# Latent attention heads: scores with keys on partitions, and float32 exponentials straight into float32 value products

## The chip, the cores and the metric

The kernel runs on one core of a Trainium2 chip. A core has five engines, each working through its own list of instructions in a fixed order: TensorE (PE, matrix products and transposes into PSUM), VectorE (DVE), ScalarE (ACT), GpSimd (POOL) and SyncE (SP), which here issues the DMA transfers. They wait for one another by semaphores. The metric is the device time of one execution in microseconds (us). The profile is that of one execution. Its page names instructions by the line of the kernel and by the tiles that they write and read (`pvm<-PTm,vt`: into `pvm` from `PTm` and `vt`). PEld is the loading of weights into TensorE, which can lie beside products.

## What is computed

One encoder layer on 1,024 positions of width 1,024, in float32: a modulated norm; one input projection; two groups of eight heads side by side, latent attention and chunk attention; one output projection; then a norm and a gated MLP. The change concerns the latent heads alone. For each of the eight heads, with queries and keys of 96 and values of 64:

```python
q = rmsnorm(q, g_mla_q[l]); k = rmsnorm(k, g_mla_k[l])      # then rotary on the last 32
s = jnp.einsum('bqhd,bkhd->bhqk', qi, k) * scale
mask = key_chunk[None, :] <= q_chunk[:, None]               # chunks of 64
s = jnp.where(mask[None, None], s, NEG_INF)
p = jax.nn.softmax(s, axis=-1)
return jnp.einsum('bhqk,bkhd->bqhd', p, v)
```

A query thus sees all keys up to the end of its own chunk of 64.

## The kernel before

The stages follow one another: norm and modulation of the input; chunk attention, with its projections and those of the latent group as fillers; latent attention; output projection and second norm; up-projection with convolution and gate, tile by tile; down-projection.

Float32 numbers go through TensorE in two pieces, a rounded one (`hi`, type fp32r, one pass per product) and a remainder (`lo`), and a product is the sum of three: hi by hi, hi by lo, lo by hi (`gemm3`). A plain float32 operand is also possible; in the profile such a product is two instructions.

A latent head is worked on in two units, `g` = 0 for the queries 0 to 511 and `g` = 1 for 512 to 1,023. For each unit `prep` makes a page of its queries and one of its keys (`qk_page`): four transposes into one PSUM bank (tag `T`, one buffer), the rounded piece by ScalarE, the remainder by VectorE. A unit has four tiles of 128 queries. `scores(i)` puts one tile's scores into PSUM with queries on partitions and up to 1,024 keys beside one another (tag `S`, two buffers, three passes, negated by the gain `gk_m`); VectorE masks the last chunk (memset) and reduces each row to its minimum; ScalarE takes the exponential with that minimum as bias and sums the rows. VectorE turns the sums into reciprocals, POOL scales the exponentials by them and rounds them to half precision, VectorE writes the remainder in half precision (`hl`), and SP issues a DMA transpose that puts keys on partitions (`PT`). `values(i)`, three tiles later (`DEPTH`), multiplies these pieces of 128 by 128 with a half-precision value tile that holds the rounded value and its remainder side by side (`vt`), so that `pv` (one PSUM bank) gets one half from the rounded values and one from the remainders. After four tiles ScalarE copies one half, VectorE adds the other, and SP writes the result to `oT_d`. The values carry a power of two worked out from the weights (`pow2_scale`).

Queries, keys and values of four heads come from `f_up(0)` and `f_up(1)`: per tile of 128 positions two small products (`qu`, `ku`) and a chain of norms and rotary steps, most of them on VectorE. These, and `f_oca`, the half of the output projection that belongs to the chunk heads (tiles `oc`), are fillers: generators from which `pace` takes a step whenever the attention work before it has paid for it, and `need` as many as a unit requires. `f_up(1)` has to be complete before the second unit of the first head. Every instruction's place on its engine is then set by a scheduler when the kernel is built, with a raised priority for scores, exponentials and values; on the chip that order is fixed.

The second half of the output projection (tiles `op`, weights `wo`) follows the last unit, needs `oT_d` of all latent heads, and reads x and the stored partial sums again.

## Time and profile before

| | us |
|---|---|
| median of 3 runs | 1458.91 (1457.85 to 1463.05) |
| the profiled execution | 1456.23 |
| its span, first to last instruction | 1454.4 |
| PE busy | 1270.4 |
| VectorE busy | 1029.9 |
| ScalarE busy | 606.5 |
| POOL busy | 770.3 |

The latent up-projections begin at about 401 us, the last value product of the latent heads ends at about 665 us, and the output projection runs until about 734 us; from there to the end it is the MLP. Busy times of different engines overlap and don't add up. The granted clock is the share of TensorE's full speed that it was given in a stretch; the mean over the span is 0.936.

### The profile page before, as it was taken

What the parts mean: (1) busy time and instruction counts of PE and PEld (TensorE: products, weight loads), DVE (VectorE), ACT (ScalarE), POOL (GpSimd) and SP (SyncE); (2) the same over time, 40 slices, a digit from 0 to 9 for tenths busy, and PEclk for the clock granted to TensorE, in tenths of its full rate; (3) what the DMA queues carried; (4) which work ended last, traced back from release to release, by engine and by line L of the source; (5) the groups of instructions that cost most, each with busy time, mean ns of one, the idle gap of its engine ahead of it and who ended that gap; (6) DMA issues with size and microseconds to landing.
All of it is one profiled execution on the core that took longest, in us unless ns stands there. A gap on an engine that the chain in (4) does not pass through costs nothing.

```text
span 1454.4 us, 20116 instructions
## 1 busy us (share of the span) xinstructions
PE 1270.4 (87%) x6836; PEld 1054.4 (72%) x6836; DVE 1029.9 (71%) x1838; ACT 606.5 (42%) x1182; POOL 770.3 (53%) x717
## 2 busy tenths in 40 slices
PE   3859988998877789886668999999999998999997
PEld 2749877887765568675546877888888887887885
DVE  6964776576688988782577778778777776566653
ACT  4544344334455555452374343443444433322331
POOL 5363544265545764333735655556655555665662
PEclk9979997999887799997878999999999999999999
DMA  7423547555522588778712322322222234447442
GB/s 283 135 70 77 130 107 144 133 119 118 114 59 55 107 162 171 149 145 261 243 41 87 116 88 101 107 82 87 88 87 87 96 130 152 152 142 241 146 145 101
DMA packets 214627, 183.85 MB, mean 126 GB/s; under 512 B 148214, under 2 KB 179066, under 8 KB 213500
## 3 DMA queue, kind: packets, MB, share of 16 engines
q1 hardware_dynamic: 214524, 182.56, 45.3%
q8 instruction: 54, 0.88, 0.3%
q14 instruction: 49, 0.40, 0.1%
HBM read 119.07 MB, written 28.84 MB: 102 GB/s over the span
## 4 chain that ended last, share of the span: by engine, by line
PE 23%; POOL 9%; DVE 8%; issue 8%; DMA 7%; ACT 1%; SPq 1%; DVEq 0%; POOLq 0%; ACTq 0%
PE p L929 5%; PE p L931 5%; PE p L930 5%; POOL wds L82 5%; DMA wu<-w_up 2%; PE dnp L1072 2%; PE dnp L1074 2%; PE dnp L1073 2%; DVE u L1007 1%; DMA wd<-w_down 1%; DVE ws L1020 1%; DVE u L1006 1%; POOL wf L82 1%; POOL we L82 1%; POOL wd L82 1%
## 5 line engine op out<-in xcount | busy, mean ns | idle before, releaser
L82 POOL TENSOR_TENSOR wds<-wd,wds 128x512 fp32r<-128x512 f32 x88 | 152.4, 1753 | 102.7 <-ACT wds L75 102.7
L82 POOL TENSOR_TENSOR wc<-ws,wc 128x512 fp32r<-128x512 f32 x22 | 65.2, 2962 | 136.7 <-ACT wc L75 136.7
L1062 DVE TENSOR_TENSOR wd<-wd,gmbc 128x1024 f32<-128x1024 f32 x44 | 68.5, 1556 | 84.1 <-DMA wd<-w_down 84.0
L1074 PE MATMUL dnp<-wds,g 128*128 128x512 f32 x308 | 119.3, 393 | 4.6 <-DVE g L82 4.6
L1072 PE MATMUL dnp<-wds,g 128*128 128x512 f32 x308 | 120.0, 392 | 1.8 <-DVE xo L1080 1.7
L75 ACT ACTIVATE wds<-wd 128x512 fp32r<-128x512 f32 x88 | 54.8, 624 | 159.1 <-PE dnp L1074 152.3
L1073 PE MATMUL dnp<-wds,g 128*128 128x512 f32 x308 | 120.1, 391 | 0.0
L71 POOL TENSOR_SCALAR hlm<-Pm,rim 128x512 f16<-128x512 f32 (+3 forms) x96 | 64.8, 685 | 78.9 <-DVE rim L684 39.7
L71 POOL TENSOR_SCALAR hlc<-Pc,ric 128x640 f16<-128x640 f32 (+2 forms) x64 | 46.2, 724 | 80.6 <-DVE ric L684 39.5
L1020 DVE TENSOR_TENSOR ws<-wu,wu 128x512 f32<-128x512 f32 x22 | 30.5, 1387 | 75.0 <-DMA wu<-w_up 75.0
L681 ACT ACTIVATE Pc<-sc,mc 128x640 f32<-128x640 f32 (+2 forms) x64 | 42.2, 660 | 91.0 <-DVE mc L670 64.1
L655 PE MATMUL sm<-mk,mq 96*128 96x512 f32 (+3 forms) x288 | 71.2, 377 | 10.2 <-ACT Pm L681 6.7
L1006 DVE SCALAR_TENSOR_TENSOR u<-c,pk,u 128x1023 f32<-128x1023 f32 x44 | 77.4, 1766 | 1.8 <-ACT u L1005 1.8
L1041 ACT ACTIVATE u<-u 128x1024 f32<-128x1024 f32 x22 | 23.4, 1063 | 132.1 <-DVE u L1007 132.1
L655 PE MATMUL sc<-k,q 64*128 64x512 f32 (+3 forms) x288 | 68.7, 365 | 10.7 <-ACT Pc L681 6.8
L82 DVE TENSOR_TENSOR g<-gr,g 128x512 fp32r<-128x512 f32 x44 | 69.8, 1588 | 11.2 <-ACT g L75 11.2
L430 DVE SCALAR_TENSOR_TENSOR aacc<-aw,cs,aacc 128x256 f32<-128x256 f32 x84 | 44.1, 525 | 47.3 <-DMA aw<-w_ada 47.0
L1005 ACT ACTIVATE u<-c,pk 128x1024 f32<-128x1024 f32 x44 | 52.3, 1236 | 56.1 <-DVE c L1037 56.1
L705 DVE SCALAR_TENSOR_TENSOR hlm<-Pm,rim,hlm 128x512 f16<-128x512 f32 (+3 forms) x96 | 68.5, 727 | 6.1 <-POOL hlm L71 5.9
L721 PE MATMUL pvm<-PTm,vt 128*128 128x128 f16 x576 | 47.2, 232 | 28.6 <-DMA PTm<-hlm 24.5
L1074 PEld LDWEIGHTS dnp<-wds,g 128*128 128x128 f32 x308 | 58.2, 189 | 18.0 <-DVE g L82 5.9
L1072 PEld LDWEIGHTS dnp<-wds,g 128*128 128x128 f32 x308 | 58.1, 189 | 15.1 <-DVE xo L1080 2.6
(366 smaller groups left out, 4281.1 us busy)
## 6 DMA issues: line engine op xcount, KB each, us to landing
wu<-w_up SPq DMA_DIRECT2D x44, 512.0 KB, 4.5
wd<-w_down SPq DMA_DIRECT2D x44, 512.0 KB, 5.1
aw<-w_ada SPq DMA_DIRECT2D x96, 128.0 KB, 2.4
g_d<-u SPq DMA_DIRECT2D x22, 512.0 KB, 2.6
gr<-g_d SPq DMA_DIRECT2D x44, 256.0 KB, 3.6
x<-x SPq DMA_DIRECT2D x16, 512.0 KB, 6.6
adaw<-w_ada_a SPq DMA_DIRECT2D x8, 1024.0 KB, 5.2
wq_r<-w_qk SPq DMA_DIRECT2D x32, 128.0 KB, 2.8
```

What stands on the lines that cost most here:

```text
L71: pool.tensor_scalar(o, i, s, 1.0, op0=MUL, op1=MUL)
L82: (pool if eng == "p" else dve).tensor_tensor(o, i, f32(hi), op=SUB)
L655: last = pe.matmul(s[:, c:c + w], qpg[rs_, a, q], kpgs[kh][rs_, b, ko:ko + w], start=(a == 0 and b == 0), stop=(a == 1))
L705: dve.scalar_tensor_tensor(hl[:, w:2 * w], pp, ri[:], hl[:, :w], op0=MUL, op1=SUB)
L929: pe.matmul(pt, sh, pg[:, 0], start=(k == 0), stop=False)
L930: pe.matmul(pt, sh, pg[:, 1], start=False, stop=False)
L931: pe.matmul(pt, sl, pg[:, 0], start=False, stop=(k == 3))
L1006: dve.scalar_tensor_tensor(u[:, 1:], c[:, :S - 1], pk[:, cv + 1:cv + 2], u[:, 1:], op0=MUL, op1=ADD)
L1062: dve.tensor_tensor(raw[:], raw[:], gmbc[:], op=MUL)
L1072: pe.matmul(pts[t][n], sh, w[n][:, 0], start=(j == 0), stop=False)
L1073: pe.matmul(pts[t][n], sh, w[n][:, 1], start=False, stop=False)
L1074: pe.matmul(pts[t][n], sl, w[n][:, 0], start=False, stop=(j == NF - 1))
```

## The change

- `qk_page` gives the key page a 97th row, of ones (from a column of ones behind each key, gain 1.0), and the query page gets a 97th row later.
- `rows_min` takes over the row minima: for each of the unit's four query tiles one pass of the rounded pieces alone, with queries on partitions as before; mask; minimum; a transpose of the column of minima into one row of a PSUM bank (tag `T`). ScalarE then copies that row, negated, into row 97 of the query page.
- `scores(x)` now puts keys on partitions and up to 512 queries beside one another, three passes, with the 97th row in the first of them, so that the minimum is taken off in the product. A unit's causal region is cut into pieces of 512, 512 (384 and 128) and 256 columns, behind four of 512 for the keys of the first half where `g` = 1. `x` counts pairs of pieces, each pair in one buffer of tag `S`. The diagonal blocks are masked, and ScalarE writes the exponential in float32, without a bias or sums.
- `values(x)`, two pairs later, multiplies these with a float32 tile that holds the values of two heads with ones between them: `pv` gets the value sums in one half and the sum of the exponentials in the other. ScalarE copies the latter, VectorE takes the reciprocal (64 by 512) and multiplies.
- The half-precision pieces, their scaling, the DMA transposes, the power of two and the remainders of the latent values are gone. The chunk heads keep all of that (`Unit`, where only the choice between the two kinds is taken out).
- A unit is begun (`begin`: pages and minima) ahead of the scores of the unit before it.

```diff
@@ -530,12 +529,6 @@
             wq.append(w)
         raw = qtile(f"wkr{gr}")
         sp.dma_start(raw[:], I["w_kvu"][gr])
-        ssw = cst.tile([P, 1], F32, name=f"sswm{gr}")
-        junk = qtile(f"wkj{gr}")
-        act.activation(junk[:, 0:256].rearrange("p (a b) -> p a b", a=4),
-                       raw[:].rearrange("p (a b) -> p a b", a=4)[:, :, NOPE:], AF.Square, accum_out=ssw[:])
-        vscale["m", gr] = pow2_scale(f"m{gr}", ssw[:], gb2[:], 1, float(KVR))
-        sc = vscale["m", gr][0]
...
-                mq[gr, t // 2] = g3([P, 2, 4, QK], F32, f"qn{gr}_{t}")
-                mk[gr, t // 2] = g3([P, 2, 4, QK], F32, f"kn{gr}_{t}")
-                mv[gr, t // 2] = G["v"].tile([P, 2, 4, 2, 64], F16, name=f"vt{gr}_{t}", tag="Gv", bufs=8)
+                mq[gr, t // 2] = g3([P, 2, 4, QK + 1], F32, f"qn{gr}_{t}")
+                mk[gr, t // 2] = g3([P, 2, 4, QK + 1], F32, f"kn{gr}_{t}")
+                pool.memset(mk[gr, t // 2][:, :, :, QK:], 1.0)
+                if gr == 0 or t >= 6:
+                    vt = G["v"].tile([P, 2, 2, 3, 64], F32, name=f"vt{gr}_{t}", tag="Gv", bufs=5)
+                    for i in range(2):
+                        mv[gr, t + i] = vt[:, i]
+                else:
+                    for i in range(2):
+                        vt = apg.tile([P, 512], F32, name=f"vt{gr}_{t + i}", tag="v16", bufs=6)
+                        mv[gr, t + i] = vt[:, :384].rearrange("p (a b c) -> p a b c", a=2, b=3)
+                for i in range(2):
+                    pool.memset(mv[gr, t + i][:, :, 1, :], 1.0)
...
-            v_t = mv[gr, t // 2][:, t % 2]
-            act.activation(v_t[:, :, 0, :], p4[:, :, NOPE:], AF.Copy, scale=sc)
-            dve.scalar_tensor_tensor(v_t[:, :, 1, :], p4[:, :, NOPE:], sc, v_t[:, :, 0, :], op0=MUL, op1=SUB)
-            q_t = mq[gr, t // 2][:, t % 2]
+            act.activation(mv[gr, t][:, :, 0::2, :], p4[:, :, NOPE:].rearrange("p (a b) d -> p a b d", a=2), AF.Copy)
...
-                    dve.memset(sv[0:64, n - 64:n], BIG)
-                    dve.tensor_reduce(m[:], sv, axis=AX.X, op=MIN)
...
-                for x, (p0, p1) in enumerate(pieces):
-                    w = p1 - p0
-                    cnt[0] += 1
-                    spare = not u.band and cnt[0] % 2
-                    if spare:
-                        hl = apg.tile([P, 1024], F16, name=f"hl{nm}_{x}", tag="v16", bufs=6)
-                    else:
-                        hl = at.tile([P, 1280], F16, name=f"hl{nm}_{x}", tag="HL", bufs=HL_BUFS)
-                    pp = pr[:, p0:p1]
-                    mode = (MODE_C if u.band else MODE_M)[cnt[0] % 4]
-                    if mode == "2":
-                        scale_pool(pp, pp, ri[:])
-                        act.activation(hl[:, :w], pp, AF.Copy)
-                        pool.tensor_tensor(hl[:, w:2 * w], pp, hl[:, :w], op=SUB)
-                    else:
-                        if mode == "1":
-                            scale_pool(hl[:, :w], pp, ri[:])
-                        else:
-                            act.activation(hl[:, :w], pp, AF.Copy, scale=ri[:])
-                        dve.scalar_tensor_tensor(hl[:, w:2 * w], pp, ri[:], hl[:, :w], op0=MUL, op1=SUB)
-                    if spare:
-                        tt = apg.tile([P, 8, P], F16, name=f"PT{nm}_{x}", tag="v16", bufs=6)
-                    else:
-                        tt = at.tile([P, 10, P], F16, name=f"PT{nm}_{x}", tag="PT", bufs=PT_BUFS)
-                    sp.dma_start_transpose(tt[:, :2 * w // P, :], hl[:, :2 * w])
-                    u.pt[i].append((tt, lo + p0 // P, w // P))
...
+    class Latent:
+
+        def __init__(u, gr, hh, g):
+            u.gr, u.hh, u.g, u.nm = gr, hh, g, f"m{gr}{hh}"
+            u.need = ["up1"] if gr or g else ["up0"]
+            d = [[(4 * g, 0)], [(4 * g + 1, 128), (4 * g + 3, 384)], [(4 * g + 2, 256)]]
+            u.pieces = [[(kb, 0)] for kb in range(4 * g)] + d
+            u.pr = {}
+
+        def prep(u):
+            gr, hh, g = u.gr, u.hh, u.g
+            u.q = qk_page(lambda j: mq[gr, (4 * g + j) // 2][:, j % 2, hh, 0:QK], f"mq{gr}{hh}_{g}", QK, "Q", 2, None)
+            k = qk_page(lambda j: mk[gr, (4 * g + j) // 2][:, j % 2, hh, :], f"mk{gr}{hh}_{g}", QK, "K", 3, gk_m[:],
+                        QK + 1)
+            pages[gr, hh, g] = k
+            u.k = [pages[gr, hh, i] for i in range(g + 1)]
+
+        def rows_min(u):
+
+            with tc.high_priority(offset=OFF_S):
+                mt = ps.tile([P, 512], F32, name=f"mt{u.nm}_{u.g}", tag="T", bufs=TB)
+                for j in range(4):
+                    n = (4 * u.g + j + 1) * P
+                    nm = f"{u.nm}_{4 * u.g + j}"
+                    s = ps.tile([P, 1024], F32, name=f"s{nm}", tag="S", bufs=2)
+                    for c in range(0, n, 512):
+                        w = min(512, n - c)
+                        pe.matmul(s[:, c:c + w], u.q[:QK, 0, j * P:(j + 1) * P], u.k[c // 512][:QK, 0, :w],
+                                  start=True, stop=True)
+                    dve.memset(s[0:64, n - 64:n], BIG)
+                    m = cst.tile([P, 1], F32, name=f"m{nm}", tag="m", bufs=4)
+                    dve.tensor_reduce(m[:], s[:, :n], axis=AX.X, op=MIN)
+                    last = pe.transpose(mt[0:1, j * P:(j + 1) * P], m[:], ident[:])
+                act.activation(u.q[QK:QK + 1, 0], mt[0:1], AF.Copy, scale=-1.0)
+
+        def scores(u, x):
+
+            cost = 0
+            with tc.high_priority(offset=OFF_S):
+                s = ps.tile([P, 1024], F32, name=f"st{u.nm}_{u.g}_{x}", tag="S", bufs=2)
+                for y, piece in enumerate(u.pieces[2 * x:2 * x + 2]):
+                    o = 512 * y
+                    for kb, c in piece:
+                        w = 512 - c
+                        ks = slice((kb % 4) * P, (kb % 4 + 1) * P)
+                        kp = u.k[kb // 4]
+                        pe.matmul(s[:, o:o + w], kp[:QK + 1, 0, ks], u.q[:QK + 1, 0, c:], start=True, stop=False)
+                        pe.matmul(s[:, o:o + w], kp[:QK, 0, ks], u.q[:QK, 1, c:], start=False, stop=False)
+                        last = pe.matmul(s[:, o:o + w], kp[:QK, 1, ks], u.q[:QK, 0, c:], start=False, stop=True)
+                        if kb >= 4 * u.g:
+                            dve.memset(s[64:128, o:o + 64], BIG)
+                        o += w
+                        cost += 3 * max(107, w / 2.4)
+                    n = o - 512 * y
+                    tag = ("P", "HL", "PT")[len(u.pr) % 3]
+                    pr = at.tile([P, 640], F32, name=f"p{u.nm}_{u.g}_{2 * x + y}", tag=tag, bufs=3)
+                    act.activation(pr[:, :n], s[:, 512 * y:o], AF.Exp, scale=-1.0)
+                    u.pr[2 * x + y] = pr
+                trail.append(last.ins)
+            return cost
+
+        def values(u, x):
+            if x == 0:
+                u.pv = ps.tile([P, 512], F32, name=f"pv{u.nm}_{u.g}", tag="pv", bufs=1)
+            cost = 0
+            with tc.high_priority(offset=OFF_V):
+                for y in (2 * x, 2 * x + 1):
+                    if y >= len(u.pieces):
+                        break
+                    o = 0
+                    for kb, c in u.pieces[y]:
+                        w = 512 - c
+                        o2 = u.hh % 2
+                        v = mv[u.gr, kb][:, u.hh // 2, o2:o2 + 2, :].rearrange("p a b -> p (a b)")
+                        last = pe.matmul(u.pv[:, c:], v, u.pr[y][:, o:o + w], start=(kb == 0),
+                                         stop=(y == len(u.pieces) - 1))
+                        o += w
+                        cost += 4 * w / 2.4
+                trail.append(last.ins)
+                if 2 * x + 2 >= len(u.pieces):
+                    dst = at.tile([P, 512], F32, name=f"o{u.nm}_{u.g}", tag="o", bufs=1)
+                    r0, r1 = (slice(64, 128), slice(0, 64)) if u.hh % 2 else (slice(0, 64), slice(64, 128))
+                    act.activation(dst[r0], u.pv[r1], AF.Copy)
+                    dve.reciprocal(dst[r0], dst[r0])
+                    dve.tensor_tensor(dst[r0], u.pv[r0], dst[r0], op=MUL)
+                    sp.dma_start(oT_d[2 * u.gr + u.hh // 2][r0, u.g * 512:(u.g + 1) * 512], dst[r0])
+            return cost
...
+    def begin(u):
+        need(u.need)
+        u.prep()
+        u.rows_min()
...
+    wait = []
+    for n, u in enumerate(lat):
+        if n + 1 < len(lat):
+            begin(lat[n + 1])
+        for x in range(2 + 2 * u.g):
+            pace(u.scores(x), R_MLA)
+            wait.append((u, x))
+            if len(wait) > 2:
+                v, y = wait.pop(0)
+                pace(v.values(y), R_MLA)
+    for v, y in wait:
+        v.values(y)
```

91 lines of the change are left out of this document (38 added, 53 removed).

## Prediction, made before the changed kernel was run

> **What bounds the kernel now.** I read the page's head first, then the table of stretches of 50 us, then the groups of the attention stage by shape, the PE timeline, and last the SP queue at the end of that stage. The profiled execution took 1456.2 us (its span and 1.8 us around it), 2.7 us under the median of 1458.9; every sum below is made against 1456.2.
>
> ```profile
> span 1454.4 us, 20116 instructions
> 400.00:450.00 50.00, 35.98 (x163) 28.20 (x162) 43.56 (x148) 26.81 (x67) 27.67 (x30) 0.76 0.30 65
> 450.00:500.00 50.00, 38.12 (x236) 31.71 (x236) 46.84 (x144) 30.04 (x70) 30.47 (x30) 0.89 0.33 65
> 550.00:600.00 50.00, 44.50 (x313) 36.29 (x314) 38.92 (x96) 25.83 (x55) 22.24 (x29) 1.00 0.83 162
> 600.00:650.00 50.00, 44.60 (x322) 36.34 (x319) 39.44 (x107) 23.54 (x51) 16.69 (x28) 0.97 0.72 145
> 1050.00:1100.00 50.00, 50.00 (x222) 41.39 (x222) 40.80 (x38) 19.96 (x28) 28.38 (x19) 1.00 0.21 74
> 401.00:514.00 113.00, 84.42 (x461) 67.81 (x461) 102.24 (x324) 63.47 (x149) 69.00 (x69) 0.81 0.37 80
> ```
>
> The columns after a stretch's length are the busy time of PE, weight loads, VectorE (DVE), ScalarE (ACT), GpSimd (POOL), then the granted clock, DMA share and GB/s. The change touches only the latent stage, from about 401 us (first up-projection) to 665 us. Until 514 us VectorE is the limit: 102.2 of 113 us busy, because the up-projection's norms and rotary steps lie beside the first heads' softmax. From 550 us on PE leads, with 44.5 of 50 us, but VectorE stays close. In the MLP, at full clock, 222 products of 512 columns fill 50 us: 0.225 us each, my PE price below.
>
> **What goes.** The groups between 400 and 665 us:
>
> ```profile
> L721 PE MATMUL pvm<-PTm,vt 128*128 128x128 f16 x576 | 47.2, 232 | 28.6 <-DMA PTm<-hlm 24.5 <-DVE om L729 4.0
> L683 DVE RECIPROCAL rim<-rsm 128x1 f32<-128x1 f32 x64 | 9.7, 152 | 7.2 <-ACT Pm L681 7.0
> L684 DVE TENSOR_SCALAR rim<-rim 128x1 f32<-128x1 f32 x64 | 9.0, 143 | 0.4
> L572 DVE SCALAR_TENSOR_TENSOR vt<-ku,vabm,vt 128x256 f16<-128x256 f32 x16 | 7.4, 464 | 1.1 <-ACT vt L571 0.9
> L705 DVE SCALAR_TENSOR_TENSOR hlm<-Pm,rim,hlm x96: 264/728/1776, 437.3 to 657.6; 128x512 f16<-128x512 f32 x48, 128x128 f16<-128x128 f32 x16, 128x256 f16<-128x256 f32 x16, 128x384 f16<-128x384 f32 x16
> L710 SPq DMA_TRANSPOSE PTm<-hlm x96: 1167/1234/2886, 437.8 to 658.7; - x96
> 632.60 1.39 PE L721 MATMUL pvm<-PTm,vt 128*128 128x128 f16 x22
> 633.80 1.38 PE L655 MATMUL sm<-mk,mq 96*128 96x256 f32 x6
> ```
>
> VectorE loses 96 low pieces (96 x 0.73 = 70 us), 64 reciprocals (9.7), 64 scalings (9.0) and 16 value remainders (7.4): 96 us. POOL loses the high pieces, SP 96 transposes (1.23 us of queue each, 118 us), PE its 24.5 us of waiting for them. Of PE work the 576 half-precision value products go: 22 of them pass in 1.20 us, 0.055 each, 31 us. The power-of-two scale of the latent values goes too; its handful of small instructions I cost at nothing.
>
> **What comes.** The score columns stay the same (keys and queries change places), and so does their PE time. Durations for the new parts:
>
> ```profile
> L456 PE MATMUL p_gm<-gmbc,ones x4: 590/592/595, 1021.3 to 1027.6; 128*128 128x512 f32 x4
> L456 PE MATMUL p_ada<-aacc,ones x8: 377/377/378, 147.1 to 248.7; 128*128 128x256 f32 x8
> L674 DVE TENSOR_REDUCE mm<-sm 128x1 f32<-128x128 f32 x8 | 2.2, 276 | 0.1
> L674 DVE TENSOR_REDUCE mm<-sm 128x1 f32<-128x1024 f32 x8 | 9.7, 1214 | 0.1
> L673 DVE MEMSET sm<- 64x64 f32 x64 | 7.2, 112 | 12.0 <-PE sm L655 11.4
> L681 ACT ACTIVATE Pm<-sm,mm 128x512 f32<-128x512 f32 x8 | 5.5, 682 | 2.9 <-DVE rim L683 1.3 <-DVE hlm L705 0.9 <-DVE mm L674 0.7
> L622 DVE SCALAR_TENSOR_TENSOR mk<-mk_ps,gk_m,mk 96x512 fp32r<-96x512 f32 x16 | 11.8, 737 | 0.7 <-ACT mk L621 0.7
> L728 ACT ACTIVATE sbm<-pvm,vabm 64x512 f32<-64x512 f32 x15 | 10.3, 684 | 6.1 <-PE pvm L721 5.9
> L729 DVE SCALAR_TENSOR_TENSOR om<-pvm,vabm,sbm 64x512 f32<-64x512 f32 x15 | 11.2, 747 | 1.1 <-ACT sbm L728 0.9
> 627.01 0.60 PE L615 MATMUL mk_ps<-ident,kn 128*96 128x128 f32 x4
> 627.36 1.62 PE L655 MATMUL sm<-mk,mq 96*128 96x512 f32 x6
> ```
>
> - Float32 value products. In the gate rows a float32 product is two instructions (4 rows for two products), and 256 more columns cost 592 - 377 = 215 ns each, so 512 columns take 2 x 0.43 = 0.86 us. All heads have 36,864 columns: 62 us on PE, 31 more than what goes.
> - Row minima: one pass over the same 36,864 columns, a third of the scores' three: 96 products, 36,864 / 512 x 0.225 = 16 us. The 64 transposes of one column each cost at most what a page's do, (627.36 - 627.01) / 4 = 0.09: 6 us. Their masks are 64 more memsets (7 us of VectorE); the reduces merely move there from the old scores. With the value products PE gains 53 us of work.
> - ScalarE: 80 exponentials (64 of 512 columns at 0.68, 16 of 256) for 64 mixed ones with an accumulator read each, and 16 row copies: within 10 us either way, on an engine half idle. POOL gets 24 memsets of ones in place of 96 passes. Both are covered; uncovered, they would cost about 10 us each.
> - The new reciprocal, 64x512, 16 times, is not in the trace. By its shape it costs 0.75 us (L729); by its operation 152 - 143 = 9 ns more for the single element of the 128x1 rows, which over 512 elements is 4.6 us if it is paid for each. The same operation is the nearer row, so I take 4.6 and keep 0.75 as the other end.
>
> The Trainium skill, VectorE: DVE Perf Modes, section on the hardware budget, says that the reciprocal is an iterative divide with a repeat count of 8; at 8 of the page's 0.96 GHz cycles per element 512 elements would take an estimated 4.3 us, which speaks against this change; the sum further down would be 1545 by it. The trace has only the 9 ns to set beside it; no run here shows a wide reciprocal.
>
> **What lies on the path.** The saving of 96 us would matter if the work interleaved freely. The built order of the changed kernel says otherwise: PE, ACT and DVE each run in a fixed order, and around every unit's end they hand a chain to one another. Last value product; ACT copy of the sums; DVE reciprocal; ACT and DVE pieces of the next unit's key page; two masks; multiply; four reduces with two more masks. Both score buffers in PSUM (tag S, two) hold minima meanwhile, so the scores of the unit already prepared start only when the third reduce frees one. A reduce is 276 ns and 134 more for each further 128 columns (the two L674 rows, seven steps apart): 1.9 us for a first-half unit, 4.05 for a second-half one. One head then takes four steps, with R the reciprocal:
> 1. Minima of a second-half unit: 0.68 + R + 0.74 + 0.22 + 0.75 + 4.05 + 0.22 = 6.7 + R; PE works about 2 us in it.
> 2. Scores and values of a first-half unit: 1,280 columns, three passes of scores 1.7 and values 2.15 on PE, then mask, exponential and hand-over about 1: 5.
> 3. Minima of a first-half unit, to its third reduce: 0.68 + R + 0.74 + 0.22 + 0.75 + 1.24 + 0.11 = 3.7 + R.
> 4. Scores and values of a second-half unit: 3,328 columns, 4.4 + 5.6 on PE, pages and first minima 0.9, and 1 of waiting for the last exponential: 12.
>
> That is 27.4 + 2R, some 28.5 + 2R with hand-overs: 30 us (R = 0.75) or 37.7 us (R = 4.6) per head, against 18 us of PE work (62 + 16 + 6 new, 49 of scores and 12 of pages, over eight heads). PE also comes back slow from such gaps:
>
> ```profile
> 663.16 1.87 PE L721 MATMUL pvm<-PTm,vt 128*128 128x128 f16 x16 [3.14 <-DMA PTm<-hlm]
> 670.50 0.79 PE L150 MATMUL op<-wo,oh 128*128 128x512 f32 x1 [5.47 <-ACT oh L75]
> 675.43 0.63 PE L151 MATMUL op<-wo,oh 128*128 128x512 f32 x1
> 675.86 0.63 PE L150 MATMUL op<-wo,oh 128*128 128x512 f32 x1
> 678.21 0.39 PE L151 MATMUL op<-wo,oh 128*128 128x512 f32 x1
> 678.44 0.39 PE L152 MATMUL op<-wo,ol 128*128 128x512 f32 x1
> 701.21 0.79 PE L150 MATMUL op<-wo,oh 128*128 128x512 f32 x1 [11.05 <-ACT oh L75]
> 676.16 7.52 SPq L588 DMA_DIRECT2D wor<-w_out  x3
> 683.74 3.73 SPq L885 DMA_DIRECT2D x<-x  x7
> ```
>
> After an idle 5.5 us the products stand 0.43 apart for 6 us, then 0.23. Two such restarts per head lie before steps 2 and 4: between 0 and 6 us, I take 3 (the 0.76 clock of the first stretch lies between half and full). So 33 or 40.7 us per head.
>
> **The sum.** The same stretch for four lines alone, in this order: low pieces (three are chunk heads'), reciprocals, scalings, minima.
>
> ```profile
> 401.00:514.00 113.00, 18.07 (x26) 0.81 0.37 80
> 401.00:514.00 113.00, 2.98 (x20) 0.81 0.37 80
> 401.00:514.00 113.00, 2.80 (x21) 0.81 0.37 80
> 401.00:514.00 113.00, 13.68 (x20) 0.81 0.37 80
> ```
>
> The up-projections end earlier. Of the 102.2 us of VectorE until 514, about 29 go (15.5 + 3 + 2.8, and the value remainders' 7.4), and about 12 come later in the new order (20 minima then are 12 first ones, 6 us less; page pieces and closing steps 6): 60 + R, at the same 90% 67 to 72 us, so it ends near 473 instead of 514. By then one unit is done and the second is in step 4. Seven heads are left, at 40.7 us 285 (the second unit's rest and the last head's missing step 3 cancel): 758. The chunk-attention half of the output projection (192 products of 512 columns, 43 us) are fillers; they fall partly into the gaps, and I add 5 us: 763, against 665.0 now (663.16 + 1.87): +98. Behind it the SP queue is freed. Today the output weights wait in it until 684 and the x loads behind them, and PE idles 11.05 us in the output projection; in the new order those weights are loaded well before. That gives 10 back (0 to 20), and the last reciprocal takes 4.6 more of the tail. In all 1456.2 + 98 - 10 + 4.6 = 1549; I say 1549 us.
>
> **Rivals.**
> - Slower by less: the reciprocal costs as its shape. Seven heads at 33 are 231; 471 + 231 + 10 of fillers = 712; +47 - 10 + 1 gives 1494 us. For it: most VectorE rows here go by their shape; against it the 9 ns.
> - Faster: PE stays packed. If minima run beside the previous unit's values, a head costs PE's 18 us and 6 of fillers; 471 + 7 x 24 = 639, 26 before today's end, and with 10 from the queue 1420 us. It decides below some 28.5 us per head, where 471 + 7 x 28.5 + 3 = 674 and the queue's 10 us cancel. For it speaks the freed VectorE and the 24.5 us of transposes' waits; against it the fixed orders and the two S buffers.
> - No change to speak of: the chain at about 28.5 us, as just worked out; 1456 us.
> - Slower by more: R = 4.6 and PE at half clock through both restarts (6 us instead of 3), with 10 us more of fillers uncovered: 1549 + 7 x 3 + 10 = 1580 us.
>
> The Trainium skill, TensorE: Matmul & The Clock Gate, Part 1, says that PE falls to half clock after an idle window of about 3.4 us; the gaps in steps 1 and 3 with the long reciprocal would pass that in every head, which is the rival just named. The rows above agree with half speed after 5.5 us of idling.
>
> **How the numbers follow.** Reciprocal by its operation 0.50 (1549), by its shape 0.30 (1494), worst 0.09 (1580), no change 0.03, faster 0.08 (1420). The range 1470 to 1590 leaves out the last two and some of the edges, 0.2 together; the likeliest case's own is 1520 to 1580. About 0.5% is what a measurement here can tell from nothing: faster 0.08, same 0.03, slower 0.89.
>
> **What would show it.** Right: a 64x512 reciprocal of 4 us or so; PE well under 80% busy in the latent stage with a clock of 0.7 to 0.85, idle mostly behind DVE reduces and S buffers; 36 us or more from one head's last product to the next's; up-projections done before 490; no 11 us gap in the output projection. Wrong: a reciprocal under 1 us, or reduces that run while the previous unit's values are still on PE, so that a head takes under 29 us; or value products dearer than 0.86 us, which would make PE itself the limit.

## The result, and the profile after

The changed kernel takes 1574.5 us (median of 4 runs, 1570.9 to 1576.5) against 1458.4 us before (1455.3 to 1463.1): ratio 1.079, 95% interval 1.0755 to 1.0826. It is slower by 116 us; 1549 was forecast, with 1470 to 1590 as the range.

The page's head and two of its groups, and the table of stretches (columns as in the prediction) for the latent stage of the kernel after:

```profile
span 1571.8 us, 19114 instructions
L788 DVE RECIPROCAL om<-om 64x512 f32<-64x512 f32 x16 | 53.6, 3347 | 44.3 <-ACT om L787 44.2
L779 PE MATMUL pvm<-pm,vt 128*128 128x512 f32 (+1 forms) x192 | 80.6, 544 | 6.3 <-ACT pm L761 6.0
550.00:600.00 50.00, 39.02 (x139) 25.99 (x140) 21.16 (x38) 12.12 (x22) 1.27 (x1) 0.77 0.08 24
600.00:650.00 50.00, 37.56 (x142) 26.18 (x141) 18.77 (x34) 13.22 (x24) 1.26 (x1) 0.80 0.07 21
484.00:798.00 314.00, 236.29 (x872) 158.90 (x870) 129.85 (x230) 94.28 (x169) 25.49 (x20) 0.81 0.14 42
```

Where PE was busy 44.5 of 50 us at a clock of 0.97 to 1.00, it is now busy 38 at 0.77 to 0.80, and VectorE, no longer short of time, 20. No engine is busy throughout: the stage waits. It ends at 798 us instead of 665 (+133); the rest of the program, 773.8 us instead of 789.4, gives 15.6 back. There the first product of each group in the output projection now waits little (the group of the stretch from 798 to 860 us: 2.6 us in all), where one gap of 11.05 us stood:

```profile
L151 PE MATMUL op<-wo,oh 128*128 128x512 f32 x64 | 26.9, 420 | 2.6 <-ACT oh L75 2.6
```

What it waits for is seen in the timeline of one unit's end (start, duration, instruction, and in brackets the idle time before it with its releaser):

```profile
720.82 1.46 PE L779 MATMUL pvm<-pm,vt 128*128 128x384 f32 x6
...
722.12 0.60 PE L616 MATMUL mk_ps<-ident,kn 128*97 128x128 f32 x4
722.62 0.59 ACT L787 ACTIVATE om<-pvm 64x512 f32<-64x512 f32 x1
...
723.24 3.35 DVE L788 RECIPROCAL om<-om 64x512 f32<-64x512 f32 x1 [2.58 <-ACT om L787]
...
724.78 0.50 PE L732 MATMUL sm<-mk,mq 96*128 96x128 f32 x2 [2.06 <-ACT mk L622]
...
726.62 0.69 DVE L82 TENSOR_TENSOR wo<-wor,wo 128x512 fp32r<-128x512 f32 x1
...
727.23 0.74 DVE L623 SCALAR_TENSOR_TENSOR mk<-mk_ps,gk_m,mk 96x512 fp32r<-96x512 f32 x1
...
728.85 0.69 DVE L789 TENSOR_TENSOR om<-pvm,om 64x512 f32<-64x512 f32 x1
...
729.57 1.69 DVE L736 TENSOR_REDUCE mm<-sm 128x1 f32<-128x640 f32 x2
...
730.54 0.37 PE L737 MATMUL mtm<-ident,mm 128*1 128x128 f32 x1 [5.27 <-DVE mm L736]
...
734.05 0.77 PE L751 MATMUL stm<-mq,mk 97*128 97x512 f32 x1 [1.32 <-DVE sm L734]
```

This is the chain that the prediction wrote out, link by link: last value product, copy, reciprocal, key piece, multiply, reduces (the masks between them left out), and only then, at 734.05, scores of a unit whose pages had long been there. PE waits 5.27 us in one piece. This end is the longest of its kind from reciprocal to scores, 10.8 us: four pieces of the output weights, fillers of 0.69 us each, stand between (the first is shown, at 726.62). At the other ends of a second-half unit it is 7.9 to 9.3. The table of waits of the stage (total, times, longest) names the same place:

```profile
PE mtm L737 <- DVE mm L736: 44.9, 13, 5.3
```

The starts of the reciprocals, with the one at 723.24 above, give the steps of a head:

```profile
678.38 3.35 DVE L788 RECIPROCAL om<-om 64x512 f32<-64x512 f32 x1 [2.46 <-ACT om L787]
...
695.70 3.35 DVE L788 RECIPROCAL om<-om 64x512 f32<-64x512 f32 x1 [2.04 <-ACT om L787]
...
743.58 3.34 DVE L788 RECIPROCAL om<-om 64x512 f32<-64x512 f32 x1 [2.05 <-ACT om L787]
...
766.53 3.34 DVE L788 RECIPROCAL om<-om 64x512 f32<-64x512 f32 x1 [2.28 <-ACT om L787]
```

From 678.38 to 695.70 lie steps 1 and 2, 17.3 us with two filler products among them; from 743.58 to 766.53 steps 3 and 4, 22.95 without fillers; from 695.70 to 723.24 steps 3 and 4 with fillers, 27.5. A head, 678.38 to 723.24, takes 44.9, which is also the mean of the six heads from 497.10 to 766.53.

### The profile page after: what moved, and what is told of

It is laid out like the page before. It is cut to its first block, busy times and chain, and to the rows that moved or that the text cites. A ratio compares the mean times of both kernels' runs of the same rounds, so it can differ in the third digit from the quotient of the medians.

```text
span 1571.8 us, 19114 instructions
## 1 busy us (share of the span) xinstructions
PE 1366.2 (87%) x6608; PEld 1090.8 (69%) x6608; DVE 1006.2 (64%) x1660; ACT 605.0 (38%) x1146; POOL 703.4 (45%) x643
## 4 chain that ended last, share of the span: by engine, by line
PE 55%; DVE 15%; DMA 12%; POOL 8%; issue 6%; ACT 3%; SPq 1%; DVEq 0%; POOLq 0%; ACTq 0%
PE p L992 8%; PE p L994 8%; PE p L993 8%; PE pvm L779 4%; POOL wds L82 4%; DMA aw<-w_ada 4%; PE sc L656 3%; PE dnp L1135 2%; PE dnp L1137 2%; PE dnp L1136 2%; DVE om L788 2%; PE stm L751 2%; PE stm L752 1%; PE stm L753 1%; DVE adacc L244 1%
## 5 line engine op out<-in xcount | busy, mean ns | idle before, releaser
L1125 DVE TENSOR_TENSOR wd<-wd,gmbc 128x1024 f32<-128x1024 f32 x44 | 65.0, 1478 | 86.2 <-DMA wd<-w_down 86.2
L761 ACT ACTIVATE pm<-stm 128x512 f32<-128x512 f32 (+1 forms) x80 | 43.6, 551 | 123.6 <-DVE stm L755 67.2
L779 PE MATMUL pvm<-pm,vt 128*128 128x512 f32 (+1 forms) x192 | 80.6, 544 | 6.3 <-ACT pm L761 6.0
L755 DVE MEMSET stm<- 64x64 f32 x64 | 7.1, 112 | 120.9 <-PE stm L753 105.6
L71 POOL TENSOR_SCALAR hlc<-Pc,ric 128x640 f16<-128x640 f32 (+2 forms) x64 | 45.7, 716 | 81.2 <-DVE ric L676 41.4
L788 DVE RECIPROCAL om<-om 64x512 f32<-64x512 f32 x16 | 53.6, 3347 | 44.3 <-ACT om L787 44.2
L82 POOL TENSOR_TENSOR cl<-cl,ch 128x512 fp32r<-128x512 f32 x8 | 10.4, 1302 | 150.5 <-ACT ch L75 149.3
L82 POOL TENSOR_TENSOR wa<-wu,wa 128x512 fp32r<-128x512 f32 x22 | 32.7, 1488 | 90.1 <-ACT wa L75 46.2
L1083 DVE TENSOR_TENSOR ws<-wu,wu 128x512 f32<-128x512 f32 x22 | 25.9, 1179 | 69.4 <-DMA wu<-w_up 69.4
```

The source lines that it names most:

```text
L82: (pool if eng == "p" else dve).tensor_tensor(o, i, f32(hi), op=SUB)
L779: last = pe.matmul(u.pv[:, c:], v, u.pr[y][:, o:o + w], start=(kb == 0), stop=(y == len(u.pieces) - 1))
L788: dve.reciprocal(dst[r0], dst[r0])
L1125: dve.tensor_tensor(raw[:], raw[:], gmbc[:], op=MUL)
```

## The experiments

Theory A (the prediction's): the order of the work around a unit's end makes a chain through VectorE, PE and ScalarE, and the chain, not any engine's work, sets the time. Theory B: the added work of PE (float32 products, minima) sets it. Within A it was open which links count: the reciprocal, the score buffers that the minima hold, the row that the scores wait for, or the place of the four minima. Each run has the kernel before timed beside it, so ratios to that are compared; 0.1% is 1.5 us. "Stage ends" is the start of the last value product in the profiled execution.

| | median, us | ratio to before (95%) | stage ends, us |
|---|---|---|---|
| after | 1574.5 | 1.079 (1.0755 to 1.0826) | 797 |
| r1 no reciprocal | 1532.4 | 1.052 (1.0466 to 1.0564) | 759 |
| r2 reciprocal behind the next scores | 1548.6 | 1.063 (1.0585 to 1.0667) | 767 |
| r3 minima in other banks | 1563.5 | 1.073 (1.0675 to 1.0783) | 784 |
| r4 no fillers in the stage | 1608.9 | 1.104 (1.0984 to 1.1096) | 774 |
| r5 no minima | 1442.0 | 0.991 (0.9876 to 0.9947) | 665 |
| r6 one-pass values | 1545.4 | 1.062 (1.0581 to 1.0657) | 770 |
| r7 r2, and the row in another bank | 1558.7 | 1.070 (1.0657 to 1.0746) | 770 |
| r8 minima that nobody reads | 1583.8 | 1.090 (1.0857 to 1.0939) | 808 |
| r9 short reduces | 1562.0 | 1.074 (1.072 to 1.0762) | 785 |
| r10 r2 and r3 together | 1587.0 | 1.092 (1.0896 to 1.0939) | 803 |
| r11 minima between the scores | 1516.1 | 1.040 (1.0366 to 1.0429) | 744 |
| r12 r11 with one-pass values | 1519.0 | 1.046 (1.0439 to 1.0489) | 738 |

### The reciprocal: left out, or moved

```diff
-                    dve.reciprocal(dst[r0], dst[r0])
```

> The changed kernel without the 16 reciprocals of 64x512 (the value sums are multiplied by the sums themselves, so the division is left out). Theory A, the chain at each unit's end: the reciprocal of 3.35 us stands in it 15 times in the stage after the up-projections and once at the end, so the time falls by 50 us or a little more (shorter gaps, fewer slow restarts): 1574 to about 1520, at most 1530. Rival B, PE's added work (float32 value products and the pass for the minima) is what costs: VectorE has time to spare, and the time stays within 8 us of 1574. Rival C, the fillers that no longer fit in: also no change.

1532.4 us, 42 less, of which 38 in the stage: 2.7 us for each of 14 unit ends, of an instruction of 3.35. That is a little short of what theory A named and far from nothing, which theory B named. The reciprocal stands on the path; but 74 us of loss are left without it.

r2 leaves the reciprocal in and moves it: ScalarE also copies the value sums (`ov`), and reciprocal, multiply and store are issued behind all masks of the next unit's scores.

```diff
-                    dve.reciprocal(dst[r0], dst[r0])
-                    dve.tensor_tensor(dst[r0], u.pv[r0], dst[r0], op=MUL)
-                    sp.dma_start(oT_d[2 * u.gr + u.hh // 2][r0, u.g * 512:(u.g + 1) * 512], dst[r0])
+                    ov = at.tile([P, 512], F32, name=f"ov{u.nm}_{u.g}", tag="ov", bufs=1)
+                    act.activation(ov[r0], u.pv[r0], AF.Copy)
+                    late.append((u, dst, ov, r0))
...
+        while late:
+            with ExitStack() as after:
+                for i in u.masks:
+                    after.enter_context(tc.issue_after(i))
+                v, *o = late.pop(0)
+                v.finish(*o)
```

> The same reciprocals, but out of the chain: ScalarE copies the values out of PSUM as well, and VectorE takes the reciprocal and multiplies only behind the last mask of the next unit's scores, by issue order. Theory A: most of the gain of the kernel without reciprocals, less the second copy of 0.6 us per unit: 1525 to 1545. Rival B: 1574 or a little more, for the added copies.

1548.6 us, 3 to 4 us short of the range. The timeline of r2 shows what the reciprocal met in its new place:

```profile
714.61 1.06 PE L616 MATMUL mq_ps<-ident,qn 128*96 128x128 f32 x4
...
716.40 3.35 DVE L794 RECIPROCAL om<-om 64x512 f32<-64x512 f32 x1
...
719.78 0.69 DVE L620 TENSOR_TENSOR mq<-mq_ps,mq 96x512 fp32r<-96x512 f32 x1
...
720.61 0.65 PE L616 MATMUL mk_ps<-ident,kn 128*97 128x128 f32 x4 [1.66 <-DVE mq L620]
```

The next query page's remainder now queues behind it, and the key page's transposes, which need the same single bank (tag `T`), behind that. r7 tested whether that bank is what binds, by putting the minima's row into one of the products' pair:

> On top of the reciprocal put behind the next unit's scores (1548.6 us), the transposed minima go to a bank of the products' pair instead of the single bank that the query and the key pages also pass through. In the trace of that run the next unit's query page is transposed only after the row of minima has been copied out (ScalarE's copy 712.19 us, transposes 714.61), and the key page only after VectorE's piece of the query page (720.50 us, transposes 720.61). Theory C (that single bank makes a chain: query page, key page, minima, one after the other) expects 1525 to 1540 us. Rival: the pages still wait for the reciprocal and the reduces on VectorE, and the products' pair is taken from the output projection's pieces: 1545 to 1555 us.

1558.7 us, no better than r2, with a stage that ends 2 us later: theory C's gain is not there, and the median lies above the rival's 1545 to 1555 too. The total hides something, though: a head takes 39.6 us instead of 41.4 (from one second-half unit's copy of the sums to the next's), and the second unit ends 12 us later, at 507.9 instead of 495.7. The same late start is in r3, where the next part shows it.

### The score buffers

```diff
-                    s = ps.tile([P, 1024], F32, name=f"s{nm}", tag="S", bufs=2)
+                    m = cst.tile([P, 2], F32, name=f"m{nm}", tag="m", bufs=4)
                     for c in range(0, n, 512):
                         w = min(512, n - c)
...
+                        s = ps.tile([P, 512], F32, name=f"s{nm}_{c}", tag="mm", bufs=2)
...
```

> The minima's scores go into the two PSUM banks of the fillers (512 columns at a time, two reduces and one small minimum for the second-half units) and not into the two score buffers; all else stays, reciprocal included. Theory A: the next unit's scores need no longer wait for the third reduce, so the minima run beside scores and values; a head then costs 28 to 34 us in place of 44, seven heads save 70 to 110 us: 1465 to 1505. Rival B: the same PE work, so 1574 within 10 us. Rival D, only the reciprocal matters and not the buffers: above 1550.

1563.5 us, 9 to 11 less by ratios and medians, with intervals that overlap: a clear miss for the expectation drawn from the prediction's sentence on the buffers. The trace says why, in two places (rows of r3):

```profile
479.49 0.80 PE L151 MATMUL oc<-wo,ch 128*128 128x512 f32 x1 [9.70 <-ACT ch L75]
...
495.43 0.79 PE L754 MATMUL stm<-mq,mk 97*128 97x512 f32 x1 [0.67 <-ACT mq L741]
...
513.76 3.35 DVE L791 RECIPROCAL om<-om 64x512 f32<-64x512 f32 x1 [4.24 <-ACT om L790]
...
720.60 3.35 DVE L791 RECIPROCAL om<-om 64x512 f32<-64x512 f32 x1 [0.55 <-ACT om L790]
...
728.80 0.37 PE L740 MATMUL mtm<-ident,mm 128*1 128x128 f32 x1 [1.25 <-DVE mm L739]
...
730.15 1.22 PE L754 MATMUL stm<-mq,mk 97*128 97x512 f32 x2 [0.98 <-ACT mq L741]
...
746.96 3.35 DVE L791 RECIPROCAL om<-om 64x512 f32<-64x512 f32 x1 [2.38 <-ACT om L790]
```

The heads do become shorter: (746.96 - 513.76) / 6 = 38.9 us instead of 44.9. They don't reach the 28 to 34 that were expected, because the scheduler now puts a second-half unit's minima directly ahead of that unit's own scores, and these wait for the row: reciprocal, reduces, transposes, row, scores. The other place is the start of the stage. The minima now share the products' pair of banks with the fillers, a filler product stands in front of them, and PE waits 9.70 us for its input; the second unit's scores start at 495.43, against 476.55 in the changed kernel, and the unit ends 17 us later. So most of the 36 us that six heads win is lost again at the stage's two ends, and the total alone makes the buffers look worth less than they are. r10 puts r2 and r3 together.

> The two changes together: reciprocal behind the next unit's scores (1548.6 alone) and minima through the products' banks (1563.5 alone). If both gains are there one beside the other: 1574 - 26 - 11 = 1537 us. If the buffers only could not show their worth because the reciprocal stood before the reduces (prediction's reason): 1515 us or less. If the buffers are not what binds: 1545 or more.

1587.0 us, slower than either and than the change itself. Only the third case (1545 or more) covers it, and nothing in that case says why it should be slower than the change. In its trace PE's own fixed order closes the chain: fillers lie between the transposes of the minima.

```profile
702.04 0.16 DVE L739 TENSOR_TENSOR mm<-mm 128x1 f32<-128x1 f32 x1
...
706.24 0.38 PE L740 MATMUL mtm<-ident,mm 128*1 128x128 f32 x2
...
707.75 0.50 PE L754 MATMUL stm<-mq,mk 97*128 97x512 f32 x1 [1.12 <-ACT mq L741]
```

The last minimum is there at 702.20, but its transpose stands behind twelve filler products on PE and runs at 706.24. This is not what puts r10 behind the change, though, for its heads are shorter: 42.3 us, against 44.9. The late start of r3 is there again (PE waits 8.85 us for a filler's input, the second unit's scores start at 494.20): the second unit ends 19 us later than in the changed kernel, six heads win 16 back, and the last head takes 8 more. What r10 would take without the late start was not tested.

### The pass as a whole, and its parts

r5 leaves the minima out. In `rows_min` only this is left (the scores are scaled by 0.01):

```diff
+                act.activation(u.q[QK:QK + 1, 0], ones[0:1, :].unsqueeze(1).to_broadcast([1, 4, P]), AF.Copy, scale=6.0)
```

> The minima pass is left out: its 20 products of a head, the 8 reduces, the transposes of the minima and the copy of the row; a constant row is written in its place, and the scores are scaled by 0.01 so that the exponentials stay finite. The work that goes is 16 + 6 us of TensorE, so a theory that counts work alone (B) gives about 1574 - 22 = 1552 us. Theory A says that the hand-overs between TensorE, VectorE and ScalarE around the minima set the period of a head (44.7 us in the mean between the reciprocals of the second units): without them the scores wait for the two pages alone, the steps behind the reciprocal go (some 5 + 12 us of hand-overs in the steps of the chain, in two units of a head), and a head takes 30 us or less where fillers run and less without: 1574 - 7 x 12 = 1490 us or less. Above 1540: the pass is not what makes the stage long. The reciprocal stays, so the value of 1459 of the kernel before is not reached by either.

1442.0 us, 132 less by the medians and 128 by the ratios, and 0.9% below the kernel before: the pass costs more than the whole loss, though its work on PE is 22 us by the prediction's prices at full clock. The stage of r5, and one of its reciprocals with its surroundings:

```profile
490.00:665.00 175.00, 160.60 (x659) 112.39 (x657) 74.53 (x111) 81.20 (x146) 21.68 (x17) 0.94 0.23 71
567.71 3.35 DVE L775 RECIPROCAL om<-om 64x512 f32<-64x512 f32 x1 [1.79 <-ACT om L774]
...
568.31 0.48 PE L738 MATMUL stm<-mq,mk 97*128 97x512 f32 x1
```

PE is busy 92% of 175 us (25 us a head) at a clock of 0.94, with all the float32 value products in it: their dearer price is not what made the change slow. And the same reciprocal holds up no scores here: the next unit's begin 0.60 us into it. The 42 us of r1 and the 132 of r5 are therefore not two terms of a sum; by these rows the reciprocal holds up PE in the changed kernel because the minima stand behind it.

r8 keeps products and reduces of the pass, in the same buffers, and drops what comes after them:

```diff
+                act.activation(u.q[QK:QK + 1, 0], ones[0:1, :].unsqueeze(1).to_broadcast([1, 4, P]), AF.Copy, scale=6.0)
...
-                    last = pe.transpose(mt[0:1, j * P:(j + 1) * P], m[:], ident[:])
-                act.activation(u.q[QK:QK + 1, 0], mt[0:1], AF.Copy, scale=-1.0)
```

> Products and reduces of the minima stay, in the same scores' buffers; the transposes of the minima, their bank and the copied row are left out, and the scores take a constant row (scaled by 0.01). So TensorE waits for a reduce only where it needs that buffer again. The prediction's reason (both buffers are held by the minima at a unit's end, so that the next scores wait for the third reduce, behind copy, reciprocal and key piece) expects that most of the loss stays: only the last transposes and the row's copy go from the steps, some 3 us of a unit, 1574 - 14 x 3 = 1530 us, and above 1515. The rival (the loss comes from TensorE's transposes that wait for VectorE's reduces in the middle of its queue, 44.9 us of waits before them in the stage, with the half clock behind each, and from the row that the scores wait for) expects 1500 us or less, near the 1442 of the kernel without the pass.

1583.8 us: nothing is won, so the transposes and the row are not the cause by themselves. Nobody reads the minima, and the scores wait all the same, now for the buffers alone (rows of r8):

```profile
701.40 3.35 DVE L786 RECIPROCAL om<-om 64x512 f32<-64x512 f32 x1 [3.40 <-ACT om L785]
...
707.82 0.56 DVE L736 TENSOR_REDUCE mm<-sm 128x1 f32<-128x384 f32 x1
...
708.43 0.79 PE L749 MATMUL stm<-mq,mk 97*128 97x512 f32 x1 [0.41 <-DVE mm L736]
484.00:808.00 324.00, 250.55 (x811) 166.08 (x810) 131.61 (x229) 94.19 (x167) 25.42 (x20) 0.76 0.13 41
```

The scores start at 708.43, where the third reduce ends, as the prediction had it. With r3 this makes the picture: buffers and row are two gates, both behind the unit's reduces. With the row's gate open and the buffers as they were (r8) a head takes 46.6 us, no less than the 44.9 before; with the buffers freed and the row in place (r3) it takes 38.9. The expectation of some 1530 was too low; in its stage PE has 61 instructions fewer than the changed kernel and is busy 14 us longer, at a clock of 0.76 instead of 0.81.

r9 shortens the reduces.

```diff
-                    dve.tensor_reduce(m[:], s[:, :n], axis=AX.X, op=MIN)
+                    dve.tensor_reduce(m[:], s[:, :64], axis=AX.X, op=MIN)
```

> Every reduce of the minima goes over 64 columns instead of 128 to 1024, so that the row isn't the minimum (the scores are scaled by 0.01 for that); all orders, buffers, transposes and waits stay. By the trace the eight reduces of a head take 0.27 + 0.41 + 0.55 + 0.69 + 0.81 + 0.94 + 1.09 + 1.23 = 6.0 us; at 0.2 us each 1.6 would be left. If they stand on the chain as a whole, 7 heads x 4.4 = 31 us go: about 1543 us (1535 to 1552), with a shorter gap before the transposes. If only the number of hand-overs counts and not their length: above 1560.

1562.0 us, just inside the second case (above 1560). A reduce took 0.22 us in the mean instead of 0.75, as intended, but the stage ends 12 us earlier, not 31. So most of what the pass costs is not the length of its reduces.

### PE's work, and the fillers

r6 stores values and exponentials in the rounded type, so that a value product is one instruction:

```diff
-                    vt = G["v"].tile([P, 2, 2, 3, 64], F32, name=f"vt{gr}_{t}", tag="Gv", bufs=5)
+                    vt = G["v"].tile([P, 2, 2, 3, 64], F32R, name=f"vt{gr}_{t}", tag="Gv", bufs=5)
...
-                    pr = at.tile([P, 640], F32, name=f"p{u.nm}_{u.g}_{2 * x + y}", tag=tag, bufs=3)
+                    pr = at.tile([P, 640], F32R, name=f"p{u.nm}_{u.g}_{2 * x + y}", tag=tag, bufs=3)
```

> Values and exponentials are stored in the rounded float32 type, so each value product is one instruction instead of two (96 fewer of 512 columns or less, about half of the 80.6 us of the value products); nothing else moves. The rounding of the products is coarser. Theory B (TensorE's work sets the period of a head) expects the whole of it: 1574 - 40 = 1534 us or less. Theory A (the chain of hand-overs sets it, and TensorE stands 25% of the stage) expects that only the products between the last exponential of a unit and its end count, two pieces of a unit with some 0.86 us of 1.7 saved, and the share of work in the other steps: 10 to 25 us, 1549 to 1564 us.

1545.4 us: 29 less by the medians, 25 by the ratios (1.7% of 1458), at or just past the upper end of theory A's 10 to 25 and short of B's 40.

r4 takes all fillers out of the stage (`R_MLA` 0.5 to 0.0).

> The pace factor of the latent units is 0, so the chunk heads' half of the output projection (192 products of 512 columns, 43 us at full clock) runs behind the last unit and not between units. It prices what the fillers cost in their places. If the gaps hid them all (as the prediction nearly had it, 5 us uncovered): 1574 + 38 = 1612. If none: 1574. From the spacing of the reciprocals (46.8 to 43.8 us per head with fillers, 43.3 and 40 without) about 24 us are uncovered: 1590 to 1600. In heads without fillers the spacing shows theory A's chain bare: 40 us per head, against 18 us of PE work, which rival B would have as the spacing.

1608.9 us, by its total near the case in which the stage hides them all. The two profiles say otherwise: the stage ends 23 us earlier (774 instead of 797), 3 of them before the up-projections' end, so about 20 us of fillers stood in the stage's length, where the prediction had 5; and behind the stage the same work takes 56 us (829.9 us from the stage's end to the span's end instead of 773.8), more than the 43 of its products at full clock. r4 also shows the heads bare: 41.0 us each, 18.0 for steps 1 and 2 and 23.0 for steps 3 and 4.

### The order alone

r11 changes nothing but the order: the next unit's minima come one or two at a time behind each pair of score pieces, the four transposes and the row at the unit's end (`rows_min` is split into the two for that).

```diff
     def begin(u):
         need(u.need)
         u.prep()
-        u.rows_min()
...
             pace(u.scores(x), R_MLA)
             wait.append((u, x))
+            if n + 1 < len(lat):
+                lat[n + 1].rows_min(range(2 * x, 2 * x + 2) if not u.g else [x])
...
+        if n + 1 < len(lat):
+            lat[n + 1].row()
```

> Nothing is left out; only the order changes. The next unit's minima are no longer issued as four in a row ahead of a unit's scores, but one or two behind each pair of score pieces, and the four transposes and the row's copy stand at the unit's end. So a pair of score pieces waits for one reduce at most before it has a buffer, and the reciprocal has no row of four reduces behind it. If what costs is the place of the four minima (products into both buffers, their reduces behind the reciprocal, the next scores behind them: 13 to 14 us of steps at each unit's end), a head goes from 44.7 us to 35 us or less: 1574 - 7 x 9 = 1511 us or less (1480 to 1515). If it is the amount of work of the pass on TensorE and VectorE, or the row that the scores wait for, wherever they stand: 1555 us or more.

1516.1 us, 1 us above the first case's range and far from the second; half of the loss is gone with all the work still there. The stage of r11, its waits for the minima, and two reciprocals six heads apart:

```profile
484.00:742.00 258.00, 221.03 (x843) 148.07 (x841) 128.91 (x225) 90.01 (x160) 22.84 (x18) 0.87 0.16 50
PE mtm L743 <- DVE mm L735: 6.8, 9, 1.1
482.52 3.33 DVE L794 RECIPROCAL om<-om 64x512 f32<-64x512 f32 x1
...
711.73 3.35 DVE L794 RECIPROCAL om<-om 64x512 f32<-64x512 f32 x1 [1.30 <-ACT om L793]
```

PE's waits for the minima's columns fall from 44.9 to 6.8 us, PE's share rises from 75 to 86%, and a head takes (711.73 - 482.52) / 6 = 38.2 us instead of 44.9. The place of the four minima and their row is thus shown to cost about 58 us of the 116. r11 still loses 4% to the kernel before, and r12 asked whether PE's work was now what is left.

> On top of the minima put between the score pieces (1516.1 us): values and exponentials in the rounded float32 type, so that each value product is one instruction (82.2 us of value products fall to some 38), with a coarser rounding. In the trace of that order TensorE is busy 221 of 258 us from 484 to 742 us, 86%, so the theory says that its work now sets the time: of the 44 us most goes, 35 or more, to 1481 us or less (1470 to 1481). With the old order the same change gave 29 of some 44. If hand-overs still set the time: 1490 us or more. The kernel before, at 1459, is not reached by either.

1519.0 us: nothing won, though half of the value instructions are gone. The theory that PE's work had become the limit, which had 1481 us or less, did not hold. The stage in r12:

```profile
484.00:742.00 258.00, 207.51 (x780) 149.63 (x781) 138.65 (x233) 95.52 (x170) 30.44 (x24) 0.76 0.17 56
```

PE is busy 207.5 us instead of 221.0 and its granted clock is 0.76 instead of 0.87: the products that are left take longer. No kernel with the minima in it beat the one before, and r5 is no way out: it leaves out the shift by the minimum, and its exponentials stay finite only because its scores are scaled by 0.01. What holds r11 back for its remaining 58 us was not settled: each head's row still stands between the last reduce and the next scores (11.1 us of PE's waits), and the clock is not full.

## Why the prediction was right, point by point

- **Direction and mechanism: right.** A chain around each unit's end, with idle PE and VectorE, at a clock that falls. The marks named for it are there: PE 75% busy at 0.81 in the stage, waits behind the reduces, 44.9 us a head, up-projections done at 484, and no gap of 11 us in the output projection. One is there in part: the reciprocal takes 3.35 us, not 4.
- **The reciprocal: right in kind, too dear.** 3.35 us instead of 4.6, nearer the end by operation than that by shape (0.75, or 0.69 for the multiply of the same tile). The 9 ns of the single element is 6.25 ns for each further column: (3347 - 152) / 511. The estimate of 4.3 us from the Trainium skill, VectorE: DVE Perf Modes, section on the hardware budget, was also too high; at that page's 0.96 GHz it measured 6.0 cycles a column, not 8. The rival of 1494 us rested on the shape's price, and r1, without any reciprocal, still took 1532: even a free one would not have brought it there.
- **The steps of a head: nearly right, with errors both ways.** With 3.35 in them, the formula gives 10.05 + 5 + 2 = 17.05 for steps 1 and 2 (half a microsecond of hand-overs and 1.5 of slow clock each) and 7.05 + 12 + 2 = 21.05 for 3 and 4; bare of fillers r4 has 18.0 and 23.0 in its middle heads, 2.9 more. Step 1 counts all four reduces, 4.05 us, where the prediction's own sentence lets the scores start behind the third, 2.84; at 734.05 they do, and the fourth begins with them. So the rest of the formula is short by 4.1.
- **The slow restarts: 3 us a head, taken from a range of 0 to 6; they came out near its upper end.** Behind the gap that ends at 750.22 products of 512 columns still stand 0.42 apart 4 us later, and 0.24 apart only from 756.46 on (rows of the changed kernel):

```profile
753.80 0.63 PE L752 MATMUL stm<-mq,mk 96*128 96x512 f32 x1
754.22 0.63 PE L753 MATMUL stm<-mq,mk 96*128 96x512 f32 x1
...
756.46 0.40 PE L752 MATMUL stm<-mq,mk 96*128 96x512 f32 x1
756.70 0.40 PE L753 MATMUL stm<-mq,mk 96*128 96x512 f32 x1
```

The granted clock was 0.51 from 750.22 to 756.20, and 0.58 from 734.05 to 740.00, behind the other gap of that head. Half speed for 5 to 6 us loses half of that at each of a head's two gaps: 5 to 6 us a head, as an estimate.
- **The fillers: the term that was mis-sized most.** 5 us were added; r4 puts 20 in the stage's length. Of the 192 products 136 fall into steps 2 and 4, where PE works, and only 56 into the gaps, because their place in PE's order is fixed.
- **Start of the stage: 11 us late.** The up-projections end at 484 us, not 473.
- **The sum.** Stage end 798 instead of 763: +11 for the start, -17.5 for 14 shorter reciprocals, +15 for fillers, +20 for 2.9 us more in the steps of seven heads; these give 29 of the 35. The other 6 I can't place by rows; the first two heads are long, 46.8 and 45.9 us between reciprocals that start at 497.10, 543.91 and 589.84. Behind the stage 15.6 us come back instead of 10 less 4.6. That makes 1573.6 for the profiled execution instead of 1549. That 1549 came as near as it did is partly luck: the reciprocal's price, 17.5 us too high, made up for a third of what the other terms of the stage lacked.
- **"Both score buffers hold minima, so the scores start when the third reduce frees one": right as a description, wrong as the only gate.** The row seen in r8 starts exactly there. Freeing the buffers shortens a head by 6 us (r3), not by the 10 to 16 that were expected, because the row of minima is a second gate behind the same reduces; r3's total shows 9 to 11 us only, because its stage starts late. Moving the reduces in the order, with the buffers as they are, shortens a head by 6.7 us without that late start (r11).
- **Float32 products on PE: right that they don't decide.** 80.6 us of value products against 62 at full clock, and r5 runs all of them in a stage as short as before.
- **The rival "slower by more" (1580 us).** The measured 1574.5 lies nearer to it than to 1549. Of its three conditions the reciprocal of 4.6 us did not come; the slow restarts came nearly in full, and the fillers cost 15 us more than in the likeliest case, where it has 10.
- **The rival "PE stays packed" (1420 us).** It needs minima that are out of the way. Without them r5 comes to 1442, at 25 us a head, close to the 24 that the rival had for PE's work.

## What to carry to other kernels

A pass that is small as work can be large as an order: a pass with some 22 us of TensorE work at full clock, its reduces in a row at the seam between two units, behind one long instruction on their engine and in front of the next unit's scores, cost 132 us. Before adding such a pass, list for the seam what is queued in front of it on each engine and who waits behind it, and put it between pieces of the running unit rather than in a row at the seam. Where two gates stand behind the same work, opening one gives back a part at most; see whether the work itself can be moved. And read an experiment by its stages as well as by its total: r3 and r7 had shorter heads than the kernels that they were made from, and lost much of it at the start of the stage, where PE waited for a filler that stood in front.

## What was not expected of the hardware

Half speed came without a long pause. In r12 (rows of PE) products of 384 columns follow one another in 0.18 us at 636 us and in 0.32 at 645.6, and between lie only two pauses, of 1.23 and 0.68 us:

```profile
636.26 0.34 PE L757 MATMUL stm<-mq,mk 97*128 97x384 f32 x1
...
636.44 0.34 PE L758 MATMUL stm<-mq,mk 96*128 96x384 f32 x1
...
642.76 0.50 PE L757 MATMUL stm<-mq,mk 97*128 97x512 f32 x1 [1.23 <-ACT mq L744]
...
644.85 0.51 PE L731 MATMUL sm<-mk,mq 96*128 96x512 f32 x1 [0.68 <-ACT mq L619]
...
645.63 0.52 PE L758 MATMUL stm<-mq,mk 96*128 96x384 f32 x1
...
645.95 0.52 PE L759 MATMUL stm<-mq,mk 96*128 96x384 f32 x1
```

The prediction had counted slow restarts only behind gaps of over 5 us. The Trainium skill, TensorE: Matmul & The Clock Gate, in its section on a second failure mode (cycling through PSUM queues), says that frequent short pauses between groups of products make the clock swing; these rows agree, while its rule of one idle window of some 3.4 us would not have foretold them. In a stage that waits, work taken off PE can thus come back as a slower clock: r6, r8 and r12 have fewer instructions on PE in the stage than the kernel they were made from, and granted clocks there of 0.71, 0.76 and 0.76 against 0.81, 0.81 and 0.87.
